# Two FFNs with seven block products for eight, one weight sum made by an accumulating transfer

## The chip, the cores and the metric

The kernel runs on one core of a Trainium2 chip. The metric is device time in microseconds of one execution, median of several. The core has five engines that each run their own instructions in order and wait for one another through semaphores: TensorE (PE, matmuls), VectorE (DVE), ScalarE (ACT), GpSimd (POOL) and SyncE (SP). Transfers are carried by 16 DMA engines; here SP issues the weight loads and GpSimd the small ones.

## The reference

One block of a streaming encoder: 256 frames of width 2048, all float32.

```python
x = x + 0.5 * swiglu_ffn(rmsnorm(x, norm_ffn1_g), ffn1_w_gate, ffn1_w_up, ffn1_w_down)   # 2048 -> 5632 -> 2048
proj = rmsnorm(x, norm_mix_g) @ w_in                                                     # 2048 -> 11264
...            # chunked band attention, chunkwise retention, gates, output projections
x = x + merged @ w_out
x = x + 0.5 * swiglu_ffn(rmsnorm(x, norm_ffn2_g), ffn2_w_gate, ffn2_w_up, ffn2_w_down)
return rmsnorm(x, norm_final_g)

def swiglu_ffn(x, w_gate, w_up, w_down):
    return (jax.nn.silu(x @ w_gate) * (x @ w_up)) @ w_down
```

Nearly all of the work is in the products of a 256-row activation with weight matrices that are each read once. The change touches the products with `w_gate` and `w_up` of the two FFNs.

## The kernel before

**Products.** A float32 product is made of three matmuls on a rounded type (fp32r): each operand is split into a high part (its rounding) and a low part (the rest), and high·high, high·low and low·high are summed in PSUM (L125 to L127). The weights are streamed in chunks of 2 x 128 rows by 512 columns, 512 KB each. For a chunk SP issues one load (`raw`, L94), ACT writes the high part (`hi`, L107), DVE subtracts to get the low part (`lo`, L108), and PE runs 12 matmuls of 512 columns: 2 row blocks by 2 frame halves by 3. A `Gemm` is a run of chunks that end in one 256x512 result in two PSUM banks.

**Order.** The order of each engine is that in which the program is written. `run` goes through the list of chunks; at each it first splits a few chunks ahead (`split_upto`), then runs what is due at this step (transposes, norms, attention pieces), then the chunk's matmuls, then what follows a finished `Gemm` (`done`). There are 4 buffers for `raw` and 5 each for `hi` and `lo`. An FFN makes 6 column blocks of 512 of the middle activation, each by a gate `Gemm` and an up `Gemm` of 8 chunks, then a part of the down product, then the other 5 blocks and the rest of the down product. There are 11 blocks in an FFN.

**Around it.** After a gate `Gemm` ACT takes SiLU out of PSUM (L374), after an up `Gemm` DVE multiplies (L379); the result is transposed on PE and split (L263, L264). After a down `Gemm` DVE adds to x (L357). The normed input is transposed and split by `Norm.put` (L322, L326, L330). x itself is loaded in quarters at the start, the last one at step 2 (L173).

## Time and profile before

| | us |
|---|---|
| median of 3 runs | 2179.64 (2179.56 to 2180.44) |
| the profiled execution, its own time | 2180.46 |
| its span, first to last instruction | 2178.4 |
| PE busy | 2167.7 |
| DVE busy | 1121.6 |
| ACT busy | 963.0 |
| GpSimd busy | 21.6 |

The granted TensorE clock of the profiled execution was 0.999 of full speed. Matmuls overlap in the records: one of 512 columns is shown with 0.39 us, while the next one starts 0.23 us later, so time is read from the starts. An instruction of DVE or ACT is likewise shown with its whole latency, and in a run of instructions the next starts a little before the end of the last.

### The profile page before, as it was taken

Reading aid. Unit: us, or ns where it says so; the run is one execution under the profiler, and the core shown is the slowest. Engines: PE = TensorE matmul, PEld = TensorE weight load, DVE = VectorE, ACT = ScalarE, POOL = GpSimd, SP = SyncE. Lnnn points to the kernel's source line nnn. Section 1 sums busy time; section 2 is a strip of 40 time slices with the busy share of each in tenths; the row PEclk is TensorE's granted clock in tenths of the full one; section 3 lists DMA queues with packets and bytes.
Section 4 is the critical chain, followed back from the end, with each engine's and each line's share of the span. In section 5 each row is a group of like instructions: output and inputs, shape, how many; then the busy total and the mean of one; then the engine's idle time right before and its main releaser. Section 6 shows DMA issues by size and latency. Waiting matters only on the chain.

```text
span 2178.4 us, 25308 instructions
## 1 busy us (share of the span) xinstructions
PE 2167.7 (100%) x9865; PEld 1802.5 (83%) x9865; DVE 1121.6 (51%) x1192; ACT 963.0 (44%) x1104; POOL 21.6 (1%) x36
## 2 busy tenths in 40 slices
PE   9999999999999999999999999999999999999998
PEld 7888888888888888888888888888888888888887
DVE  5544554445545544556655555554544544444554
ACT  6444433444444444454444444454444433444443
POOL 0000000000000000000000000000000000000000
PEclk9999999999999999999999999999999999999999
DMA  7655655666665555555555555556656556666554
GB/s 253 208 188 187 222 192 194 212 188 190 187 209 184 184 190 187 175 163 178 167 177 190 188 192 192 185 183 194 193 184 193 189 194 212 189 192 191 186 192 137
DMA packets 213512, 414.51 MB, mean 190 GB/s; under 512 B 12864, under 2 KB 13616, under 8 KB 213392
## 3 DMA queue, kind: packets, MB, share of 16 engines
q1 hardware_dynamic: 211424, 406.90, 57.9%
q0 software_dynamic: 1824, 5.93, 0.9%
q8 instruction: 77, 1.26, 0.2%
q14 instruction: 43, 0.35, 0.0%
q10 hardware_dynamic: 144, 0.07, 0.0%
HBM read 409.17 MB, written 3.67 MB: 190 GB/s over the span
## 4 chain that ended last, share of the span: by engine, by line
PE 99%; issue 0%; DMA 0%; ACT 0%; DVE 0%; POOL 0%; POOLq 0%; ACTq 0%
PE acc L125 32%; PE acc L126 32%; PE acc L127 32%; PE f2a0p L269 0%; PE f1a0p L269 0%; PE n1p L322 0%; DMA grows<-in_norm_ffn_g_dram 0%; PE f2a6p L269 0%; PE f1a6p L269 0%; PE mgp L269 0%; PE nmp L322 0%; PE n2p L322 0%; PE as L479 0%; PE rs L537 0%; PE av L514 0%
## 5 line engine op out<-in xcount | busy, mean ns | idle before, releaser
L108 DVE TENSOR_TENSOR lo<-raw,hi 128x1024 fp32r<-128x1024 f32 (+1 forms) x769 | 938.8, 1223 | 1014.0 <-ACT hi L107 1013.6
L107 ACT CAST hi<-raw 128x1024 fp32r<-128x1024 f32 (+1 forms) x769 | 808.2, 1052 | 1106.8 <-PE acc L127 1081.8
L125 PE MATMUL acc<-hi,nmh 128*128 128x512 f32 x704 | 277.8, 395 | 0.0
L125 PE MATMUL acc<-hi,n1h 128*128 128x512 f32 x704 | 276.2, 392 | 0.0
L125 PE MATMUL acc<-hi,n2h 128*128 128x512 f32 x704 | 274.8, 390 | 0.0
L126 PE MATMUL acc<-lo,n1h 128*128 128x512 f32 x704 | 274.7, 390 | 0.0
L127 PE MATMUL acc<-hi,n1l 128*128 128x512 f32 x704 | 274.6, 390 | 0.0
L127 PE MATMUL acc<-hi,nml 128*128 128x512 f32 x704 | 274.5, 390 | 0.0
L126 PE MATMUL acc<-lo,nmh 128*128 128x512 f32 x704 | 274.1, 389 | 0.0
L127 PE MATMUL acc<-hi,n2l 128*128 128x512 f32 x704 | 274.0, 389 | 0.0
L126 PE MATMUL acc<-lo,n2h 128*128 128x512 f32 x704 | 273.9, 389 | 0.0
L127 PEld LDWEIGHTS acc<-hi,n1l 128*128 128x128 f32 x704 | 132.4, 188 | 27.6
L127 PEld LDWEIGHTS acc<-hi,nml 128*128 128x128 f32 x704 | 132.2, 188 | 27.9
L125 PEld LDWEIGHTS acc<-hi,n1h 128*128 128x128 f32 x704 | 132.6, 188 | 27.3
L126 PEld LDWEIGHTS acc<-lo,n1h 128*128 128x128 f32 x704 | 132.4, 188 | 27.3 <-DVE lo L108 0.4
L127 PEld LDWEIGHTS acc<-hi,n2l 128*128 128x128 f32 x704 | 132.2, 188 | 27.5
L126 PEld LDWEIGHTS acc<-lo,n2h 128*128 128x128 f32 x704 | 132.2, 188 | 27.1
L125 PEld LDWEIGHTS acc<-hi,n2h 128*128 128x128 f32 x704 | 132.2, 188 | 27.0
L126 PEld LDWEIGHTS acc<-lo,nmh 128*128 128x128 f32 x704 | 132.3, 188 | 26.2
L125 PEld LDWEIGHTS acc<-hi,nmh 128*128 128x128 f32 x704 | 132.3, 188 | 26.2
L125 PE MATMUL acc<-hi,f2a0h 128*128 128x512 f32 x192 | 74.8, 390 | 0.0
L125 PE MATMUL acc<-hi,f1a0h 128*128 128x512 f32 x192 | 74.8, 389 | 0.0
(266 smaller groups left out, 2107.3 us busy)
## 6 DMA issues: line engine op xcount, KB each, us to landing
raw<-in_ffn_w_up_dram SPq DMA_DIRECT2D x176, 512.0 KB, 3.5
raw<-in_ffn_w_down_dram SPq DMA_DIRECT2D x176, 512.0 KB, 3.6
raw<-in_w_in_dram SPq DMA_DIRECT2D x176, 512.0 KB, 3.5
raw<-in_ffn_w_gate_dram SPq DMA_DIRECT2D x175, 512.0 KB, 3.5
raw<-in_w_out_dram SPq DMA_DIRECT2D x32, 512.0 KB, 3.7
raw<-in_w_out_att_dram SPq DMA_DIRECT2D x16, 512.0 KB, 4.3
raw<-in_w_out_ret_dram SPq DMA_DIRECT2D x16, 512.0 KB, 4.3
xall<-in_x_dram SPq DMA_DIRECT2D x3, 512.0 KB, 7.5
```

The costliest lines, as they stand in the source:

```text
L107: nc.scalar.copy(hi[:, p, :], raw[:, p, :])
L108: nc.vector.tensor_sub(lo[:, p, :], raw[:, p, :], hi[:, p, :].bitcast(F32))
L125: nc.tensor.matmul(acc, ahi[:, ts], whi[:, cs], start=first, stop=False)
L126: nc.tensor.matmul(acc, ahi[:, ts], wlo[:, cs], start=False, stop=False)
L127: nc.tensor.matmul(acc, alo[:, ts], whi[:, cs], start=False, stop=last)
```

## The change

In both FFNs the gate and up products of column blocks 1 to 10 are made together, as a 2 x 2 by 2 x 2 block product with seven products in place of eight. A is the normed activation: two frame halves of 128 rows, and the 2048 inner rows in two interleaved halves. B has gate and up as its two block columns, and the same inner halves: B11 and B21 are parts of gate, B12 and B22 of up. The sums are

- of A, made once per norm (`add_up`): s5, s7, s6, s3;
- of B, made for each block (`Strassen.step`): T1 = B11 + B12, T2 = T1 + B22, T2 - B11, T4 = T2 + B21.

A block is a group of 16 steps in four phases of four (`jc` 0 to 3), each step on a piece of 256 rows by 512 columns of each block: phase 0 multiplies a00·B11 and s5·T1, phase 1 s6·T2 and s3·B22, phase 2 s7·(T2 - B11) and a01·B21, phase 3 a11·T4. So a step of phases 0 to 2 has two weight operands, 12 matmuls, two `hi` and two `lo`; one of phase 3 has one operand and 6 matmuls. Standard chunks (up of block 0, then down) are woven in between, one at each D of `WOVEN`; a group with its D steps is `ppppD ppDppD pDpDpDpD ssssD`.

**T1** is made by a transfer: GpSimd issues a DMA from the tile with B11 (`k`) to the tile with B12 (`x`) that adds (L478). The other sums are DVE instructions: L513 (T2), L517 (T2 - B11), L521 (T4). B11 and B12 are kept in 8 tiles of the activation pool (`KEPT`), 4 `k` and 4 `x`; these are all that one group needs, and the next group's loads take the tiles as phases 2 and 3 free them.

Other edits: `hi` and `lo` have 4 buffers each, not 5, and a step's split waits until there is room for all its operands; PSUM has 4 banks for `acc`, 2 for `std`, 2 for `side`, where it had 4 and 4; some attention tiles move to the activation pool; the norms write a scaled copy first and split from that; the last `Gemm` keeps 2 steps (`TAIL`), not 4, for its three closing parts.

Three places of the order matter below. In names, `z104` is a group (that of block 5 of the first FFN), `z104k0` and `z104x0` are its tiles of `jc` 0, and `hiz104130` is the `hi` of group `z104`, phase 1, `jc` 3, operand 0.

ACT before, where one `Gemm` ends and chunks of later ones are split:

```order
L107 CAST hi58_1315<-raw58_1247 128x1024
L107 CAST hi59_1333<-raw59_1265 128x1024
L374 ACTIVATE f1g30_1351<-acc48_0_1195,n1rstd_88 128x512
L374 ACTIVATE f1g31_1353<-acc48_1_1196,n1rstd_88 128x512
L107 CAST hi60_1355<-raw60_1283 128x1024
L107 CAST hi61_1375<-raw61_1301 128x1024
```

ACT now, from the last step of phase 0 to the first two of phase 1:

```order
L498 CAST hiz104031_2604<-z104x3_2479 128x1024
L114 CAST hi108_2621<-raw108_2482 128x1024
L553 ACTIVATE z104s1_2639<-z104a_2567,n1rstd_88 128x512
L553 ACTIVATE z104s5_2641<-z104c_2574,n1minus_89 128x512
L498 CAST hiz104100_2644<-rawz10410_2484 128x1024
L498 CAST hiz104101_2647<-z104x0_2364 128x1024
L498 CAST hiz104110_2669<-rawz10411_2486 128x1024
```

Two copies out of PSUM stand ahead of the splits of phase 1, as two stood ahead of a later chunk's split before; what now follows them is only one D step ahead of PE.

DVE before, in a gate `Gemm`, one instruction to a chunk:

```order
L108 TENSOR_TENSOR lo38_925<-raw38_836,hi38_924 128x1024
L108 TENSOR_TENSOR lo39_943<-raw39_854,hi39_942 128x1024
L108 TENSOR_TENSOR lo40_961<-raw40_874,hi40_960 128x1024
L108 TENSOR_TENSOR lo41_979<-raw41_894,hi41_978 128x1024
L108 TENSOR_TENSOR lo42_997<-raw42_928,hi42_996 128x1024
```

DVE now, from the last step of phase 1 to the first of phase 2:

```order
L513 TENSOR_TENSOR z104x3_2479<-z104x3_2479,rawz10413_2652 128x1024
L501 TENSOR_TENSOR loz104130_2734<-rawz10413_2652,hiz104130_2733 128x1024
L501 TENSOR_TENSOR loz104131_2737<-z104x3_2479,hiz104131_2736 128x1024
L115 TENSOR_TENSOR lo114_2756<-raw114_2677,hi114_2755 128x1024
L561 SCALAR_TENSOR_TENSOR z104s2_2773<-z104c_2574,n1minus_89,z104s2_2773 128x512
L517 TENSOR_TENSOR z104k0_2362<-z104x0_2364,z104k0_2362 128x1024
L521 TENSOR_TENSOR z104x0_2364<-z104x0_2364,rawz10420_2695 128x1024
L501 TENSOR_TENSOR loz104200_2779<-rawz10420_2695,hiz104200_2778 128x1024
L501 TENSOR_TENSOR loz104201_2782<-z104k0_2362,hiz104201_2781 128x1024
L115 TENSOR_TENSOR lo116_2789<-raw116_2718,hi116_2788 128x1024
```

A D step has one of these instructions, a step of phase 1 three and one of phase 2 four, and the reading of a PSUM bank (L561) stands between the phases.

SP before, at the start:

```order
L94 DMA raw5_157<-in_ffn1_w_gate_dram 128x2x512
L94 DMA raw6_177<-in_ffn1_w_gate_dram 128x2x512
L94 DMA raw7_206<-in_ffn1_w_gate_dram 128x2x512
L173 DMA xall_77<-in_x_dram 128x2x512
L94 DMA raw8_234<-in_ffn1_w_up_dram 128x2x512
```

SP now:

```order
L108 DMA raw7_221<-in_ffn1_w_gate_dram 128x2x512
L108 DMA z8k0_223<-in_ffn1_w_gate_dram 128x2x512
L108 DMA z8x0_225<-in_ffn1_w_up_dram 128x2x512
L108 DMA z8k1_228<-in_ffn1_w_gate_dram 128x2x512
L108 DMA z8x1_230<-in_ffn1_w_up_dram 128x2x512
L108 DMA z8k2_233<-in_ffn1_w_gate_dram 128x2x512
L108 DMA z8x2_235<-in_ffn1_w_up_dram 128x2x512
L108 DMA z8k3_238<-in_ffn1_w_gate_dram 128x2x512
L108 DMA z8x3_240<-in_ffn1_w_up_dram 128x2x512
L219 DMA xall_77<-in_x_dram 128x2x512
```

The last quarter of x, which followed chunk 7, now follows the eight kept tiles of the first group.

The diff, cut to what these parts speak of:

```diff
 MASKED = -1e30
 
 RAW_BUFS = 4
-SPLIT_BUFS = 5
-ACT_TILES = 26
-TAIL = 4
+SPLIT_BUFS = 4
+KEPT = 8
+ACT_TILES = 30
+TAIL = 2
 AHEAD = (2, 3)
+BY_DMA = ("T1",)
+HALF_K = D // P // 2
+LEAD = 8
+EARLY = 3
+WOVEN = "ppppD" "ppDppD" "pDpDpDpD" "ssssD"
+WOVEN_LAST = "pDppDpD" "pDpDpDpD" "pDpDpDpD" "ssDssD"
 WARM = (6, 3)
 TAIL_PARTS = ((0, slice(0, NB)), (1, slice(0, NB // 2)), (1, slice(NB // 2, NB)))
...
+        def __call__(self, k, t):
+            ts = slice(t * P, (t + 1) * P)
+            return self.hi[k // 4][:, k % 4, ts], self.lo[k // 4][:, k % 4, ts]
...
+                if self.sums:
+                    nc.vector.tensor_scalar_mul(self.minus, self.rstd, -1.0)
+
+        def split_to(self, key, js, src):
+            if key not in self.part:
+                self.part[key] = [
+                    apool.tile([P, HALF_K, P], F32R, tag="act", name=f"{self.name}{key}{i}") for i in "hl"
+                ]
+            hi, lo = self.part[key]
+            nc.scalar.copy(hi[:, js, :], src)
+            nc.vector.tensor_sub(lo[:, js, :], src, hi[:, js, :].bitcast(F32))
...
+            j = 4 * (b // 2) + 2 * half
+            for t in range(NT):
+                src = raw[:, 2 * half : 2 * half + 2, t * P : (t + 1) * P]
+                self.split_to(f"a{t}{b % 2}", slice(j, j + 2), src)
+                    for n in range(2):
+                        later(1 + n, lambda n=n: self.add_up(b // 2, n))
...
+        def add_up(self, p, n):
...
+                s5, s7, s6, s3 = self.f
+                nc.vector.tensor_sub(s5, a22, a21)
+                nc.vector.tensor_sub(s7, a11, a21)
+                nc.vector.scalar_tensor_tensor(s6, s5, -1.0, a11, op0=ALU.mult, op1=ALU.subtract)
+                nc.vector.scalar_tensor_tensor(s3, s6, -1.0, a12, op0=ALU.mult, op1=ALU.subtract)
+            for i in (2 * n, 2 * n + 1):
+                self.split_to(self.SUMS[i], slice(4 * p, 4 * p + 4), self.f[i])
...
+    class Strassen:
...
+        def steps(self):
+            return [self.step(phase, jc) for phase in range(4) for jc in range(HALF_K // KC)]
...
+            def load_first():
+                self.kept[jc] = kept_tile("k")
+                fetch(self.kept[jc], self.w[0], self.rows(0, jc), self.col[0])
+
+            def load_second():
+                self.x[jc] = kept_tile("x")
+                fetch(self.x[jc], self.w[1], self.rows(0, jc), self.col[1])
+                if "T1" in BY_DMA:
+                    nc.gpsimd.dma_start(self.x[jc], self.kept[jc], accum_op=ALU.add)
+
+            def load_raw():
+                made["raw"] = weights_tile(f"raw{name}")
+                i = 2 - phase
+                fetch(made["raw"], self.w[i], self.rows(1, jc), self.col[i])
...
+            def two(first, second):
+
+                tiles = []
+                for i, raw in enumerate((first, second)):
+                    hi = wpool.tile([P, KC, NB], F32R, tag="hi", bufs=SPLIT_BUFS, name=f"hi{name}{i}")
+                    lo = wpool.tile([P, KC, NB], F32R, tag="lo", bufs=SPLIT_BUFS, name=f"lo{name}{i}")
+                    nc.scalar.copy(hi, raw)
+                    tiles.append((raw, hi, lo))
+                for raw, hi, lo in tiles:
+                    nc.vector.tensor_sub(lo, raw, hi.bitcast(F32))
+                return [(hi, lo) for _, hi, lo in tiles]
+
+            def prep():
+                x = self.x[jc]
+                if phase == 0:
+                    if "T1" not in BY_DMA:
+                        nc.vector.tensor_add(x, x, self.kept[jc])
+                    made["w"] = two(self.kept[jc], x)
+                elif phase == 1:
+                    raw = made["raw"]
+                    if "T2" not in BY_DMA:
+                        nc.vector.tensor_add(x, x, raw)
+                    made["w"] = two(raw, x)
+                elif phase == 2:
+                    raw, k = made.pop("raw"), self.kept.pop(jc)
+                    nc.vector.tensor_sub(k, x, k)
+                    if "T4" in BY_DMA:
+                        nc.gpsimd.dma_start(x, raw, accum_op=ALU.add)
+                    else:
+                        nc.vector.tensor_add(x, x, raw)
+                    made["w"] = two(raw, k)
+                else:
+                    made["w"] = [split(self.x.pop(jc), name)]
+
+            def products():
+                w = made["w"]
+                if phase == 0:
+                    self.product("a", "a00", jc, w[0], True, False)
+                    self.product("c", "s5", jc, w[1], True, False)
+                elif phase == 1:
+                    self.product("a", "s6", jc, w[1], False, False)
+                    self.product("c", "s3", jc, w[0], False, True)
+                elif phase == 2:
+                    self.product("a", "s7", jc, w[1], False, False)
+                    self.product("b", "a01", jc, w[0], True, True)
+                else:
+                    self.product("a", "a11", jc, w[0], False, True)
+                if jc == n - 1:
+                    self.end(phase)
+
+            loads = [("kept", load_first), ("kept", load_second)] if phase == 0 else [("raw", load_raw)]
+            frees = [[], ["raw"], ["raw", "kept"], ["kept"]][phase]
+            return Step(self, 0, loads if phase < 3 else [], prep, frees, 1 if phase == 3 else 2, products,
+                        early if phase == 1 and "T2" in BY_DMA else None)
+
+        def end(self, phase):
+
+            norm, acc, copy = self.norm, self.acc, self.copy
+
+            def copied(key, bank, scale):
+                copy[key] = tmp_tile(f"{self.name}{key}", "qk", 4)
+                nc.scalar.activation(copy[key], acc[bank], AF.Copy, scale=scale)
+
+            if phase == 0:
+                copied("s1", "a", norm.scale(0))
+                copied("s5", "c", norm.minus_scale(1))
+            elif phase == 1:
+                copied("s2", "a", norm.minus_scale(0))
+                r = copy["s2"]
+                nc.vector.scalar_tensor_tensor(r, acc["c"], norm.minus_scale(0), r, op0=ALU.mult, op1=ALU.add)
+                self.evict(0, 1, r)
+            elif phase == 2:
+                r = copy["s5"]
+                nc.vector.scalar_tensor_tensor(r, acc["a"], norm.minus_scale(1), r, op0=ALU.mult, op1=ALU.add)
+                self.evict(1, 1, r)
+                r = copy["s1"]
+                nc.vector.scalar_tensor_tensor(r, acc["b"], norm.scale(0), r, op0=ALU.mult, op1=ALU.add)
+                self.evict(0, 0, r)
+            else:
+                self.evict(1, 0, None, acc["a"])
...
+        queue = plain(0)
+        for pair in range((nblocks + 1) // 2):
+            queue += down(pair)
+        queue = [(job, k) for job in queue for k in range(0, job.nk, KC)]
+
+        def next_standard(n):
+            for job, k in queue[:n]:
+                steps.append(standard(job, k))
+            del queue[:n]
+
+        next_standard(LEAD)
+        for b in range(1, nblocks):
+            group = paired(b).steps()
+            for what in WOVEN if b < nblocks - 1 else WOVEN_LAST:
+                if what == "D":
+                    next_standard(1)
+                else:
+                    steps.append(group.pop(0))
+            assert not group
+        next_standard(len(queue))
+
+    n1 = Norm("n1", gains[:, 0, :], True)
+    nm = Norm("nm", gains[:, 1, :], False)
+    n2 = Norm("n2", gains[:, 2, :], True)
```

336 lines of the change are left out of this document (216 added, 120 removed).

## The prediction, as it was written before the changed kernel was run

> **What bounds the kernel now.** I read the page's busy times first, then the chain of waits that ended last.
>
> ```profile
> PE 2167.7 (100%) x9865; PEld 1802.5 (83%) x9865; DVE 1121.6 (51%) x1192; ACT 963.0 (44%) x1104; POOL 21.6 (1%) x36
> PE 99%; issue 0%; DMA 0%; ACT 0%; DVE 0%; POOL 0%; POOLq 0%; ACTq 0%
> ```
>
> PE sets the end; DVE and ACT work half the time. Third, the timeline of a stretch in the first FFN (start, duration, engine, line; idle before in brackets), which gives the rhythm and the hand-overs.
>
> ```profile
> 702.38 0.39 PE L125 MATMUL acc<-hi,f1a6h 128*128 128x512 f32 x1
> 702.58 1.05 ACT L107 CAST hi<-raw 128x1024 fp32r<-128x1024 f32 x1 [1.67 <-PE acc L127]
> 702.61 0.39 PE L126 MATMUL acc<-lo,f1a6h 128*128 128x512 f32 x1
> ...
> 703.67 1.23 DVE L108 TENSOR_TENSOR lo<-raw,hi 128x1024 fp32r<-128x1024 f32 x1 [1.50 <-ACT hi L107]
> ...
> 705.10 0.39 PE L125 MATMUL acc<-hi,f1a6h 128*128 128x512 f32 x1
> ```
>
> Twelve matmuls start between 702.38 and 705.10: 2.72 us a chunk, 0.227 us a matmul. ACT starts 0.20 us after PE has gone on from the chunk that held its buffer; DVE starts 0.04 us after ACT's end (702.58 + 1.05 = 703.63). Each chunk needs 1.23 us of DVE in 2.72. How dense DVE and ACT can go is seen where several follow one another (x is their count, the duration is of all):
>
> ```profile
> 36.53 1.26 ACT L374 ACTIVATE f1g<-acc,n1rstd 128x512 f32<-128x512 f32 x2
> 37.69 2.95 ACT L107 CAST hi<-raw 128x1024 fp32r<-128x1024 f32 x3
> 38.77 4.63 DVE L108 TENSOR_TENSOR lo<-raw,hi 128x1024 fp32r<-128x1024 f32 x4 [3.15 <-ACT hi L107]
> 56.66 1.40 DVE L379 SCALAR_TENSOR_TENSOR f1g<-acc,n1rstd,f1g 128x512 f32<-128x512 f32 x2
> ```
>
> In a row a DVE instruction of 1024 takes (4.63 - 1.23)/3 = 1.14 us. The groups by line and shape give the rest (busy, mean ns of one):
>
> ```profile
> L379 DVE SCALAR_TENSOR_TENSOR f1g<-acc,n1rstd,f1g 128x512 f32<-128x512 f32 x22 | 15.4, 743 | 0.0
> L357 DVE SCALAR_TENSOR_TENSOR xall<-acc,xall 128x512 f32<-128x512 f32 x38 | 24.4, 682 | 0.0
> L374 ACT ACTIVATE f1g<-acc,n1rstd 128x512 f32<-128x512 f32 x22 | 15.0, 689 | 9.9 <-PE acc L127 9.9
> ```
>
> So in a row 0.66 us (1.40 - 0.74) for a scaled eviction on DVE, 0.60 for the other ones of 512 (0.68 less the same 0.08), and 0.57 for one on ACT (1.26 - 0.69).
>
> **What PE loses.** Twenty groups (ten a FFN) have 168 matmuls each where two Gemms had 192: 480 x 0.227 = 108.8 us off the chain that sets the end. With nothing else this gives 2180.5 - 108.8 = 2071.7 on the profiled execution's own time.
>
> **What DVE gains.** A group has 28 splits for 16, and 12 sums (T2, T2 - B11, T4; four of each): 24 more instructions of 1024, 480 in all, 547 us at 1.14. That fits into the whole span, but it falls into the groups. A group with its 8 D steps, put-in-middle included, phase by phase:
>
> - phase 0 (`ppppD`): PE 5 x 2.72 + 8 transposes (0.87, row below) = 14.5. DVE 9 x 1.14 + 3 x 0.60 + 2 x 0.60 = 13.3.
> - phase 1 (`ppDppD`): PE 16.3. DVE 14 x 1.14 + 0.66 = 16.6.
> - phase 2 (`pDpDpDpD`): PE 21.8. DVE 20 x 1.14 + 2 x 0.60 = 24.0.
> - phase 3 (`ssssD`): PE 8.2. DVE 5 x 1.14 + 2 x 0.66 + 0.60 = 7.6.
>
> ```profile
> 104.69 0.87 PE f1a0p L269 x8
> ```
>
> PE 60.8 us, DVE 61.5: DVE goes from half busy to as busy as PE. Nor can it save up time: `hi` and `lo` have four buffers and a step takes two, so it is at most two steps (5.4 us) ahead, less where a buffer comes free late. Three waits are then PE's.
>
> 1. Phase 0 to 1. ACT reads both banks before it splits for phase 1, and the second closes with PE's last product of phase 0. From there 0.20 + 0.57 (second eviction) + 1.05 (`hi`) + 0.04 + 1.14 (first `lo`) + 1.23 (second, which the product takes first) + 0.04 = 4.27 us; PE has a D step and one matmul, 2.72 + 0.23 = 2.95, so it waits 1.3. In the next step DVE's sum and two `lo` take 1.14 + 1.14 + 1.23 = 3.5 against 2.72: 0.8 more. Together 2.1.
> 2. Phase 1 to 2. L561 stands ahead of phase 2's instructions on DVE and waits for the end of phase 1; behind it are T2 - B11, T4 and both `lo`, and for these PE: 0.20 + 0.66 + 3 x 1.14 + 1.23 + 0.04 = 5.55, less 2.95, 2.6.
> 3. Phase 2 itself: 24.0 - 21.8 = 2.2.
>
> Phase 3 costs nothing extra, since its evictions stand behind the first `lo` of the phase and PE has a D step and that step's 1.36 us meanwhile. A group thus takes 60.8 + 6.9 = 67.7 us, and 20 groups add 138. A bound from below is each phase at its longer engine, 14.5 + 16.6 + 24.0 + 8.2 = 63.3, 2.5 a group. From above, every extra semaphore that stands on DVE's way could cost its 0.04 on some 40 instructions, 1.6 us a group, 32 in all. I take 138, because the waits follow from the order of single engines.
>
> **T1 by transfer.** It takes four DVE instructions, 4.6 us, out of each group, else DVE would be at 66. GpSimd is free for it. Its price is not in the trace; the nearest rows are GpSimd's transfers of the same 512 KB, beside the weights' queue (median us to landing):
>
> ```profile
> q1 hardware_dynamic: 211424, 406.90, 57.9%
> raw<-in_ffn_w_up_dram SPq DMA_DIRECT2D x176, 512.0 KB, 3.5
> biasT<-rel_ext POOLq DMA_DIRECT2D x2, 512.0 KB, 6.1
> decay<-in_decay_dram POOLq DMA_DIRECT2D x2, 512.0 KB, 7.1
> ```
>
> The queue moves 406.9 MB in 57.9% of 2178 us, 323 GB/s, so reading the target as well adds 1.6 us: 7.7 to 8.7. Below it is 6.1, a plain one; above 14.2, both ends done in turn. The cover: the group's last kept tile is free when phase 3's last `lo` ends; up to the fourth x of the next phase 0 DVE has eight more instructions of 1024 and five of 512, 12.1 us, less ACT's 1.1; 3.5 go to the load, 7.5 are left. At 8.7 it is 1.2 late, which phase 0's surplus (14.5 - 13.3) takes in. So I cost it at nothing, but without that cover each us is 20.
>
> [...]
>
> **Start, end, the rest.** x's last quarter is now behind eight kept tiles on SP.
>
> ```profile
> 17.40 0.46 SPq L173 DMA_DIRECT2D xall<-in_x_dram  x1
> L322 PE MATMUL n1p<-id_sb,xall x32: 270/272/476, 6.0 to 29.6; 128*128 128x128 f32 x32
> DMA to landing us min/median/max: 4.1/5.5/9.4
> ```
>
> Eight tiles are 4.2 MB, 13 us at 323 GB/s. Before, it was issued at 17.4 and landed 4 to 9 us later; its transposes stand shortly before 29.6, so 4 us or so are spare and PE waits about 9 (0 if the loads go faster, 13 without any slack). The first groups also have the sums of A on DVE, about 16 instructions of 512 (10 us) a norm, under the first eight chunks in which DVE has 12 us free: I take 4 for both norms (0 to 20). At the end two steps in place of four halve the cover of the closing work, parts of 2.7 us become 1.36: 2 us (0 to 3). The mixer's moved tiles and PSUM banks lie under PE at DVE 50% busy: nothing, at most a copy of 0.6 us at each of a few transposes.
>
> Sum: 2180.5 - 108.8 + 138 + 9 + 4 + 2 = 2224.7. The median of the runs is 0.8 below the profiled execution, so **2224 us**, 2.0% slower.
>
> **The rivals.**
>
> A. The waits don't come, and a group ends at its longer engine phase by phase: 2071.7 + 50 + 15 = 2137, faster. For it: ACT has 40% of a group to spare (36 casts of 0.95 and some 6 us of evictions in 67), and DVE's sums are ready early. Against: L561 and the evictions stand in order ahead of what PE needs next. At 2 us of wait a group in place of 6.9 it is still faster; the sides change at 4.7 (108.8 - 15 over 20).
>
> B. T1 lands late. At 14.2 us it is 6.7 late, 5.5 after the slack, and all of it is PE's: 2224 + 110 = 2334; at 11 us, half way, 2270. For it: no row shows the price, and the next group's tiles are loaded only when this one frees them. Against: 6.1 and 7.1 for a like transfer.
>
> C. The waits shrink by a third, as PE's and DVE's delays overlap: 20 x 4.7 + 15 - 108.8 = 0, about 2180, no change.
>
> D. The clock. PE now stands still for up to 2.6 us at a time, and after an idle start it runs at half speed:
>
> ```profile
> 10.20 0.63 PE L127 MATMUL acc<-hi,n1l 128*128 128x512 f32 x1
> 10.62 0.63 PE L125 MATMUL acc<-hi,n1h 128*128 128x512 f32 x1
> core 0: 2178.4 us, clock 0.999
> ```
>
> 0.42 us from start to start, against 0.23. If one such wait a group brought 3 us at half speed, as the start has, that is 1.5 x 20 = 30: 2254. [...]
>
> **How the numbers follow.** The forecast's mechanism 0.61, with its own range 2205 to 2250; B 0.17; A 0.10; C 0.07; D 0.05. Eight in ten reach from 2190 (the forecast with 5.2 us of waits a group) to 2290 (T1 at 12 us). Repeated runs here differ by 0.04%, and I call a change told from none at 0.2%, 4.4 us. Faster: A and a third of C, 0.12; same: a third of C and a little of the edges, 0.04; slower: the rest, 0.84.
>
> **What would show it.** In the groups' stretches DVE at 90% or more busy, PE's matmul starts with gaps; by the waits PE's matmuls released by DVE `lo` of L501, most time at the first step of phase 2 (2.6 us each), then phase 1 (1.3 and 0.8); a period of 67 to 68 us from one group's first product to the next one's. ACT's `hi` of x waiting for GpSimd's DMA would show B; a granted clock under 0.98 D; a period under 65 A. A gap of some 9 us near 26 us would bear out the start. The forecast is wrong if DVE has idle time between the phases that PE does not share.

## The result, and the profile after

The changed kernel takes **2314.6 us** (2309.4 to 2315.4) against 2179.6: 1.0614 times as long, 95% interval 1.0595 to 1.0632. The direction was forecast, the size was not: 2224 was the number and 2290 the upper end. Executions of one kernel agree within 0.5%, except one of experiment 2 at 7446 us, which its ratio leaves out. The profiled execution has a span of 2313.6 us; its page gives busy times and the chain of waits that ended last:

```profile
PE 2156.8 (93%) x9337; PEld 1732.8 (75%) x9337; DVE 1742.8 (75%) x1830; ACT 1243.1 (54%) x1468; POOL 90.5 (4%) x116
PE 57%; DVE 19%; DMA 11%; issue 6%; ACT 4%; SPq 0%; POOL 0%; ACTq 0%; DVEq 0%; POOLq 0%
```

PE went from 100% of the span to 93% and from 99% of the chain to 57%. That DVE would stand in the chain was forecast; the **11% of DMA** was not. In one group, from its first product at 564.8 us to the next one's at 636.8 (72.0 us, forecast 67.7), the view of waits (who waited for what: us in all, times, longest) says for PE:

```profile
PE z176a L123 <- DVE loz L501: 3.7, 3, 1.9
PE z176c L122 <- ACT hiz L498: 1.8, 1, 1.8
PE z176c L123 <- DVE loz L501: 0.8, 1, 0.8
PE z176a L122 <- ACT hiz L498: 0.5, 1, 0.5
```

the same view for DVE:

```profile
DVE loz L501 <- ACT hiz L498: 6.8, 3, 4.6
DVE z176s L561 <- PE z176c L124: 1.8, 1, 1.8
...
```

and for ACT, among others:

```profile
...
ACT hiz L498 <- DMA z176x<-z176k: 5.0, 1, 5.0
...
```

This row is the sign named for rival B: ACT stands 5.0 us for an adding transfer, DVE 4.6 us behind ACT, and PE pays 1.8 + 0.8 at the fourth product of s5 (gaps of 1.9 and 1.03 us between matmul starts, 9.4 us into the group). DVE stands 2 us longer there than PE; idle time of DVE that PE doesn't share was the forecast's own sign of being wrong. The first and fourth rows of PE are the forecast waits. By matmul starts these are, in a group without late T1 (of experiment 2 below), 1.22 + 0.70 (forecast 1.3 + 0.8), 0.63 + 2.17 (2.6) and 1.42 (2.2): 6.1 us for 6.9.

Why T1 is late shows in the group at 493.6 us. The transfers of its kept tiles (KB each, median us to landing):

```profile
z152k<-in_ffn_w_gate_dram SPq DMA_DIRECT2D x4, 512.0 KB, 8.1
z152x<-in_ffn_w_up_dram SPq DMA_DIRECT2D x4, 512.0 KB, 8.8
z152x<-z152k POOLq DMA_DIRECT2D x4, 512.0 KB, 9.4
```

The medians hide the last load. Of the loads of x and the additions into them the view of their tile says, from issue to landing:

```profile
DMA to landing us min/median/max: 6.5/9.3/16.0
```

The queues between 470 and 505 us (packets, MB, share of the 16 engines):

```profile
q1 hardware_dynamic: 3657, 7.03, 56.1%
q0 software_dynamic: 576, 2.10, 30.1%
```

GpSimd's timeline there:

```profile
480.33 0.86 POOL L478 DMA_DIRECT2D z152x<-z152k  x1 [54.99 <-DMA z152x<-in_ffn_w_up_dram]
482.94 0.86 POOL L478 DMA_DIRECT2D z152x<-z152k  x1 [1.76 <-DMA z152x<-in_ffn_w_up_dram]
485.64 0.86 POOL L478 DMA_DIRECT2D z152x<-z152k  x1 [1.84 <-DMA z152x<-in_ffn_w_up_dram]
495.81 0.86 POOL L478 DMA_DIRECT2D z152x<-z152k  x1 [9.31 <-DMA z152x<-in_ffn_w_up_dram]
```

The transfer itself takes about what was estimated (9.4 for 7.7 to 8.7; the medians of the twenty groups are 8.5 to 10.0). What is late is what it adds to: SP issues the eight kept loads in a row between 472.7 and 479.2, and the last x, issued at 479.2, lands at 495.3, 16 us later, where 3.5 were assumed. In these 35 us a load takes 0.561 x 35 / 13.4 = 1.5 us of all 16 engines (7.03 MB are 13.4 loads) and an adding transfer 0.301 x 35 / 4 = 2.6. The first three additions run while the last loads wait, and between them they hold up the fourth's operand: GpSimd stands 9.3 us for it. The fourth T1 lands at 503.3, 24.0 us after the load was issued.

The cover, the time from that load's issue to the use of the tile, is not as it was forecast either. The last load is issued when the last `lo` of phase 2 has ended (478.00 + 1.22), not the last of phase 3, which ends 8.8 us later (484.49 + 3.50):

```profile
478.00 1.22 DVE L501 TENSOR_TENSOR loz<-z128k,hiz 128x1024 fp32r<-128x1024 f32 x1
479.24 0.37 SPq L108 DMA_DIRECT2D z152x<-in_ffn_w_up_dram  x1
484.49 3.50 DVE L115 TENSOR_TENSOR loz<-z128x,hiz 128x1024 fp32r<-128x1024 f32 x3 [0.25 <-ACT hiz L114]
```

At the start the wait for x's last quarter is 16.2 us where 9 were forecast (view of one tile: who waited for x, us, times):

```profile
  DMA xall<-in_x_dram: 16.2, 1
```

The granted clock is 0.972 in place of 0.999. DVE is busy 87% of two groups (125.4 of 144.1 us, row in experiment 4), under the 90% that the forecast named.

### The profile page after: what moved, and what is told of

It reads as the page before. It is cut to its first block, busy times and chain, and to the rows that moved or that the text cites. A ratio compares the mean times of both kernels' runs of the same rounds, so it can differ in the third digit from the quotient of the medians.

```text
span 2313.6 us, 25633 instructions
## 1 busy us (share of the span) xinstructions
PE 2156.8 (93%) x9337; PEld 1732.8 (75%) x9337; DVE 1742.8 (75%) x1830; ACT 1243.1 (54%) x1468; POOL 90.5 (4%) x116
## 3 DMA queue, kind: packets, MB, share of 16 engines
q1 hardware_dynamic: 211424, 406.90, 55.1%
## 4 chain that ended last, share of the span: by engine, by line
PE 57%; DVE 19%; DMA 11%; issue 6%; ACT 4%; SPq 0%; POOL 0%; ACTq 0%; DVEq 0%; POOLq 0%
PE acc L122 13%; PE acc L124 13%; PE acc L123 13%; DVE loz L501 7%; ACT hiz L498 3%; DVE lo L115 3%; DVE xall L587 1%; DMA z128x<-z128k 1%; DMA z632x<-z632k 1%; DMA z512x<-in_ffn_w_up_dram 1%; DMA z56x<-in_ffn_w_up_dram 1%; DMA z104x<-in_ffn_w_up_dram 1%; DMA z704x<-in_ffn_w_up_dram 1%; DMA z680x<-z680k 1%; DMA z584x<-in_ffn_w_up_dram 1%
## 5 line engine op out<-in xcount | busy, mean ns | idle before, releaser
L115 DVE TENSOR_TENSOR lo<-raw,hi 128x1024 fp32r<-128x1024 f32 (+1 forms) x449 | 545.7, 1220 | 311.5 <-ACT hi L114 310.7
L114 ACT CAST hi<-raw 128x1024 fp32r<-128x1024 f32 (+1 forms) x449 | 469.6, 1047 | 346.6 <-PE acc L124 312.5
L501 DVE TENSOR_TENSOR loz<-rawz,hiz 128x1024 fp32r<-128x1024 f32 x160 | 195.1, 1219 | 33.2 <-ACT hiz L498 33.2
L498 ACT CAST hiz<-rawz 128x1024 fp32r<-128x1024 f32 x160 | 167.1, 1045 | 57.5 <-PE acc L124 29.8
L122 PE MATMUL acc<-hi,nma00h 128*128 128x512 f32 x176 | 70.6, 401 | 0.0
L122 PE MATMUL acc<-hi,nma01h 128*128 128x512 f32 x176 | 70.1, 398 | 0.0
L124 PE MATMUL acc<-hi,nma00l 128*128 128x512 f32 x176 | 68.7, 390 | 0.0
L124 PE MATMUL acc<-hi,nma01l 128*128 128x512 f32 x176 | 68.6, 390 | 0.0
L122 PE MATMUL acc<-hi,nma10h 128*128 128x512 f32 x176 | 68.6, 390 | 0.0
L123 PE MATMUL acc<-lo,nma00h 128*128 128x512 f32 x176 | 68.6, 390 | 0.0
```

Source lines behind the costliest of these rows:

```text
L114: nc.scalar.copy(hi[:, p, :], raw[:, p, :])
L115: nc.vector.tensor_sub(lo[:, p, :], raw[:, p, :], hi[:, p, :].bitcast(F32))
L122: nc.tensor.matmul(acc, ahi, whi, start=first, stop=False, **more)
L123: nc.tensor.matmul(acc, ahi, wlo, start=False, stop=False, **more)
L124: nc.tensor.matmul(acc, alo, whi, start=False, stop=last, **more)
L498: nc.scalar.copy(hi, raw)
```

## The experiments

Each is an edit of the changed kernel; before takes 2178.6 to 2179.4 us beside them.

**1. T1 on DVE.**

```diff
-BY_DMA = ("T1",)
+BY_DMA = ()
```

> B11+B12 is made by DVE in place of the adding transfer; nothing is left out. Theory 1 (the fourth T1 of a group lands 2 to 3 us late, and that is what the transfer costs): the PE wait of 1.2 to 2.2 us + 1.03 at 9.4 us into a group goes (-3.0 x 20 = -60 us), but DVE has 4 x 1.14 = 4.6 us more in phase 0, 17.9 against PE's 14.5, so +3.4 x 20 = +68: 2300 to 2330 us, no verdict on the transfer as a whole, but the waits of ACT hiz on z..x go. Theory 2 (the loads and the weights' queue are what is slow, and T1 is only the place where it shows): the gap at 9.4 us stays and DVE's load comes on top: 2380 us. Theory 3 (DVE has slack in phase 0, the forecast's DVE count is too high): 2250 us.

Measured: 2303.1 us, 1.0566 (1.0550 to 1.0582), 0.5% **faster** than with the transfer. ACT waits for no adding transfer any more; a group takes 71.55 us. The row of the stretch 554.5 to 626.1 (length; busy us and instructions of PE, its weight loads, DVE, ACT, GpSimd; clock; DMA share; GB/s):

```profile
554.50:626.10 71.60, 64.08 (x275) 49.62 (x274) 67.27 (x64) 40.00 (x43) 0.00 (x0) 1.00 0.51 176
```

DVE is busy 94% of it. Theory 1 holds: two prices of the same size.

The loads are issued here as in the changed kernel, eight in a row, with no addition beside them. From issue to landing the four of `z152x` take:

```profile
DMA to landing us min/median/max: 6.4/8.8/9.9
```

The last takes 9.9 us in place of 16.0. So of the 12.5 us over the assumed 3.5 the loads among themselves make 6.4, and the group's first three additions 6.1.

**2. No T1.** The sum is left out, so the s5 product takes B12 alone.

```diff
-                if "T1" in BY_DMA:
-                    nc.gpsimd.dma_start(self.x[jc], self.kept[jc], accum_op=ALU.add)
```

> T1 is left out: neither transfer nor DVE makes B11+B12, so the product that should take the sum takes B12 alone. Theory 1 (late T1 costs 3 us a group, and the clock falls after it): the gap at 9.4 us goes, -60 us, and with it the half-clock windows that follow it, 12 or so of the 25 at some 1.7 us each, -20: 2235 us, a group at 68 to 69. Theory 2 (the fourth x is late because eight loads of 512 KB stand in a row, transfer or not): the gap shrinks by less than half, 2285 us or more. Theory 3 (the clock falls for the waits at phase 2 alone): the gap goes, the number of half-clock windows stays, 2255 us.

> The kernel without T1 once more (neither transfer nor DVE makes B11+B12; the product that should take the sum takes B12 alone), for its trace: it took 2250 us. Theory 1: the gap at 9.4 us of a group is gone, the waits at 0 to 1 (1.2 + 0.7), 1 to 2 (0.6 + 2.2) and in phase 2 (1.4) stay, a group takes 68.5 us, and the half-clock windows that are left follow the wait at phase 2. Theory 2: the gap is there, smaller, and ACT's hiz waits for the load.

Measured: 2250.3 us, 1.0322 (1.0305 to 1.0340), and 2249.0 in a single further execution, whose trace is read here. PE's waits in a group and its stretch:

```profile
PE z176a L123 <- DVE loz L499: 4.6, 4, 1.9
PE z176a L122 <- ACT hiz L496: 0.5, 1, 0.5
...
537.70:606.00 68.30, 63.06 (x274) 49.81 (x272) 62.53 (x60) 40.42 (x44) 0.00 (x0) 1.00 0.54 185
```

The gap at 9.4 us is gone and the forecast's waits are left, with a group at 68.35 us; DVE is busy 92% of it. **All that the transfer of T1 costs is 2314.6 - 2249.0 = 65.6 us.** Nothing waits for T1 here, so the trace shows the cover, from the issue of the group's last load to the `hi` of its fourth x:

```profile
454.67 0.37 SPq L108 DMA_DIRECT2D z152x<-in_ffn_w_up_dram  x1
474.77 1.06 ACT L496 CAST hiz<-z152x 128x1024 fp32r<-128x1024 f32 x1 [0.30 <-PE z152c L124]
```

These are 20.1 us, where the forecast had 12.1 - 1.1 = 11.0; from the last `lo` of phase 3, where it began to count, they are 11.3. In the changed kernel load and addition take 24.0, 4 us more than the cover. Part of the 65.6 is at the start: x's last quarter is waited for 8.8 us here (and in experiment 1), not 16.2, so 7.4 come from the first group's adding transfers, which are in flight beside it (x's quarter is issued at 23.4 us, they from 25.3 on).

**3. x's last quarter first.**

```diff
     load_x(2 * NB, 3 * NB)
+    load_x(3 * NB, 4 * NB)
 ...
-    at(2, lambda: load_x(3 * NB, 4 * NB))
```

> x's last quarter is loaded right behind its third, ahead of the eight kept tiles. Theory 1 (the quarter behind the kept tiles costs the 16.2 us that PE waits for it): -16 us, less up to 1.6 us by which the kept tiles come later: 2297 us. Theory 2 (the start's loads are bound by bandwidth, the wait only moves to the chunks or the first T1): within 4 us of 2314.

Measured: 2301.3 us, 1.0558 (1.0543 to 1.0574): 13.3 of the 16.2 us. PE has no wait for x, and the first group starts at 41.4 us in place of 53.4.

**4. Matmuls in the waits.**

```diff
+FILL = (4, 7)
 ...
+                    if jc == n - 1:
+                        self.fill(FILL[0])
                     self.product("c", "s5", jc, w[1], True, False)
 ...
-                    self.product("a", "s7", jc, w[1], False, False)
+                    self.product("a", "s7", jc, w[1], False, False, FILL[1] if jc == 0 else 0)
```

`fill(n)` issues n matmuls of 512 columns into a bank that is not yet in use; in the call of `product` they stand behind its first matmul.

> Matmuls that need no new data go into two of the waits of a group and write a bank that is not yet in use: 4 (0.9 us) ahead of the fourth x's product of phase 0, 7 (1.6 us) between the first product's hi and lo at phase 2. 220 matmuls more, 50 us of PE's work. Theory 1 (the granted clock falls to a half for 3.41 us after a stretch of 3.41 us in which PE stood still for 2.0 us or more; the fillers lie in waits and cost nothing): almost no half-clock windows between 70 and 2300 us, which have cost some 45 us; DVE has used some of it to catch up, so -25 to -45: 2270 to 2290 us. Theory 2 (the clock falls for another reason, such as power, with the load): it falls as often or more, 2314 us or more. Theory 3 (the waits are not waits for data, fillers come on top): +50, 2365 us.

What it tests is seen in the changed kernel in three stretches of 3.41 us, behind late T1 of the group above:

```profile
574.83:578.24 3.41, 1.16 (x4) 0.77 (x5) 1.94 (x2) 2.58 (x3) 0.00 (x0) 1.00 0.00 0
578.24:581.65 3.41, 3.41 (x10) 2.63 (x9) 1.99 (x3) 2.09 (x3) 0.00 (x0) 0.50 0.49 145
581.65:585.07 3.42, 3.35 (x15) 2.42 (x14) 3.42 (x4) 1.69 (x3) 0.00 (x0) 1.00 0.39 114
```

PE stands for most of the first, runs at half clock in the second, at full in the third. Laid out from the trace's clock changes and matmul starts, 632 such stretches at full clock lie between 30 us and the end: in the 28 that are followed by half clock PE stood 1.99 us or more, in the 604 others at most 2.09.

Measured: 2312.6 us, 1.0613 (1.0597 to 1.0628): no difference from the change. The two groups from 564.8 to 708.9 in the changed kernel:

```profile
564.80:708.90 144.10, 131.54 (x547) 103.03 (x545) 125.40 (x119) 80.02 (x87) 6.85 (x8) 0.96 0.68 207
```

and the same stretch with the fillers (its two groups lie from 566.0 to 708.7):

```profile
564.80:708.90 144.10, 133.87 (x578) 104.85 (x577) 126.25 (x120) 80.65 (x87) 6.85 (x8) 1.00 0.67 210
```

The clock is 1.00 here in place of 0.96, and 0.988 over the span in place of 0.972: it goes with PE's standing still, as theory 1 has it, and the fillers cost nothing (2312.6 us against 2314.6); but the 25 to 45 us that I expected of it don't come. The half-clock stretches stand in a group whose end DVE sets: while PE is slow, DVE gets ahead, and a later wait shrinks (by matmul starts the 1.22 us wait of phase 1 is 0.24 behind the half-clock stretch above, and the 1.42 us wait in phase 2 is missing where such a stretch stands ahead of it). Experiment 6 shows this more closely.

**5. The eviction at phase 1's end a step later.**

```diff
-                nc.vector.scalar_tensor_tensor(r, acc["c"], norm.minus_scale(0), r, op0=ALU.mult, op1=ALU.add)
-                self.evict(0, 1, r)
+                def close():
+                    nc.vector.scalar_tensor_tensor(r, acc["c"], norm.minus_scale(0), r, op0=ALU.mult, op1=ALU.add)
+                    self.evict(0, 1, r)
+
+                later(1, close)
```

> The eviction of c at the end of phase 1 (L561 on DVE) is issued a step later, so that T2-B11, T4 and the two lo of phase 2's first step and the lo of the D step stand ahead of it. Theory 1 (the wait at phase 1 to 2 comes from that order): DVE no longer idles 1.85 us there, and the PE waits of 0.6 + 2.2 us go, of which DVE's 0.66 for the eviction comes back in phase 2: between -1.85 x 20 = -37 and -2.8 x 20 = -56, 2258 to 2277 us. Theory 2 (DVE's amount of work sets the group, and the wait only moves on to the next steps of phase 2): 2300 us or more.

Measured: 2273.0 us, 1.0431 (1.0416 to 1.0447), -41.6. DVE's wait at L561 is gone; PE's waits in a group:

```profile
PE z176a L123 <- DVE loz L501: 2.3, 3, 1.3
PE z176c L122 <- ACT hiz L498: 1.4, 1, 1.4
PE z176c L123 <- DVE loz L501: 0.8, 1, 0.8
```

The 0.63 + 2.17 at phase 2's first step become 0.88 at a later one: 1.9 us less a group, of the 2.1 (41.6 / 20) that were gained, as theory 1 has it (DVE's 0.66 comes back). The wait that the forecast priced highest is a matter of order on one queue.

**6. k0, x0, k1, x1 loaded earlier.**

```diff
+    for i in range(LEAD, len(transfers) - 7):
+        rings = "".join(r[0] for r, _ in transfers[i : i + 10])
+        if rings == "rrkkkkkkkk":
+            d3, d4, *kept = transfers[i : i + 10]
+            transfers[i : i + 10] = kept[:2] + [d3] + kept[2:4] + [d4] + kept[4:]
```

> The loads of a group's first two pairs of kept tiles are issued two and one places earlier on SP: k0, x0 ahead of the last two standard tiles of the group before, k1, x1 between them. Same bytes, same transfers. Theory 1 (T1 is late because eight loads and four adding transfers share 16 engines within 25 us; the adding transfer takes 2.7 to 2.9 us of all of them, a load 1.35): about 5 us of it are done before the bunch, the fourth T1 lands 4 us earlier and the gap of 1.2 to 2.2 + 1.03 us goes: 2255 to 2275 us. Theory 2 (the adding transfer's own 7.5 to 10 us is what is late): the last load is as late as before, 2300 us or more.

Measured: 2267.1 us, 1.0400 (1.0382 to 1.0417), -47.5. PE's waits in a group, and two groups' stretches, each from its first product to the next one's:

```profile
PE z176a L123 <- DVE loz L501: 3.4, 3, 1.9
PE z176a L122 <- ACT hiz L498: 0.5, 1, 0.5
...
549.30:617.70 68.40, 64.52 (x276) 51.10 (x273) 62.64 (x61) 40.58 (x44) 3.43 (x4) 0.98 0.69 216
1800.90:1869.30 68.40, 63.18 (x276) 49.91 (x274) 62.63 (x61) 40.52 (x44) 3.44 (x4) 1.00 0.68 215
```

The same bytes and the same 80 additions, and late T1 is gone: 68.35 us, what a group takes without T1. An addition takes here about what it took before (group medians of 7.4 to 9.1 us); the last load of `z152x` lands after 9.7 us in place of 16.0, and load and addition together take 18.6, inside the cover of 20.1. So the lateness was the **bunch**, loads and additions on the same engines at once, not the transfer's own time: in experiment 1 the same loads, alone, land early enough to leave an addition its time, and here the same additions come in time with the loads spread. And the group with a half-clock stretch (0.98) takes as long as that without (1.00), 68.4 us each: the clock costs nothing here.

**7. T4 on GpSimd.**

```diff
-                        nc.vector.tensor_add(x, x, raw)
+                        nc.gpsimd.tensor_add(x, x, raw)
```

> The sum T4 of phase 2 (four of 128x1024 a group) is made by GpSimd in place of DVE. Theory 1 (DVE's work sets phase 2): 4 x 1.14 = 4.6 us less for DVE, the wait in phase 2 (1.4) goes and that at phase 1 to 2 falls by 1.1: -2.5 x 20 = -50, 2265 us. Theory 2 (only the order at the hand-overs costs): -1.1 x 20 = -22, 2293 us. Theory 3 (DVE runs slower while GpSimd works on the same memory, or GpSimd's sum comes too late for phase 3): 2315 us or more.

Measured: 2369.3 us, 1.0872 (1.0855 to 1.0888), 55 us slower. The groups by line (busy, mean ns of one | idle before): GpSimd's sum, and the `lo` that DVE makes beside it:

```profile
L521 POOL TENSOR_TENSOR z176x<-z176x,rawz 128x1024 f32<-128x1024 f32 x4 | 12.4, 3098 | 40.2 <-DVE z176k L517 32.1 <-ACT hiz L498 4.7 <-DMA rawz<-in_ffn_w_gate_dram 3.5
...
L501 DVE TENSOR_TENSOR loz<-z176k,hiz 128x1024 fp32r<-128x1024 f32 x8 | 15.7, 1956 | 0.5 <-ACT hiz L498 0.3
```

The same `lo` in the changed kernel:

```profile
L501 DVE TENSOR_TENSOR loz<-z176k,hiz 128x1024 fp32r<-128x1024 f32 x8 | 9.7, 1218 | 0.0
```

The mean of 1956 mixes two kinds. Five of the eight take 1.22 us, three take 3.0 to 3.3, each beside a sum on GpSimd; the first pair in the timeline:

```profile
617.13 3.20 POOL L521 TENSOR_TENSOR z176x<-z176x,rawz 128x1024 f32<-128x1024 f32 x1 [32.05 <-DVE z176k L517]
...
618.16 3.26 DVE L501 TENSOR_TENSOR loz<-z176k,hiz 128x1024 fp32r<-128x1024 f32 x1
```

Theory 3. In these three the subtraction ends 1.09 us behind the sum, near the 1.14 of one in a row, as if it had waited the sum out. In the whole kernel 62 subtractions of L501 are that long, 2.0 us over their 1.22 each, 124 us; what DVE saves is 80 x 1.14 = 91. T1 is no later with this edit: ACT waits 90 us in all for adding transfers, 96 in the changed kernel. How the 55 us come out of these 33 more of DVE's time isn't taken apart.

**8. The three edits 3, 5 and 6 together.**

> The three edits that each made it faster, together: k0, x0, k1, x1 loaded earlier (alone -47.5 us), the eviction of c a step later (-41.6), x's last quarter ahead of the kept tiles (-13.3). Theory 1 (they take away different waits): the gains add up, 2314.6 - 102.4 = 2212 us, a group at 66.3. Theory 2 (behind them stands DVE's amount of work in phase 2, which takes part of it back): 2225 to 2240 us.

Measured: 2212.9 us, 1.0152 (1.0136 to 1.0167); the sum of the single gains gave 2212. A group:

```profile
521.60:588.00 66.40, 62.87 (x274) 49.81 (x273) 62.45 (x60) 40.44 (x44) 3.42 (x4) 1.00 0.71 222
```

The three gains add up, so the three edits take away different waits. DVE is busy 94%.

**9 and 10. T4 by transfer too, and T4 alone by transfer**, both on top of 8.

```diff
-BY_DMA = ("T1",)
+BY_DMA = ("T1", "T4")        # 9
+BY_DMA = ("T4",)             # 10
```

> As the kernel with the three edits, and the sum T4 of phase 2 is made by an adding transfer too. Theory 1 (DVE's work in phase 2 is what is left: it falls by 4.6 us a group, and the waits of 1.4 and 0.9 us there go): -2.3 x 20 = -46 against the three, 2166 us, and faster than the kernel before. Theory 2 (80 more transfers that take 2.8 us of all 16 engines each collide with the kept tiles' loads and with T1, which comes late again): no gain, 2212 us or more. Theory 3 (the transfer holds the raw buffer longer than DVE did, and the four raw buffers run out): PE waits for raw loads in phase 2, 2230 us or more.

> As the kernel with the three edits, but DVE makes T1 and an adding transfer makes T4. Theory 1 (each sum costs what DVE's queue has room for at its place): T1 on DVE brings the waits of 1.9 + 0.7 in phase 0, +51, T4's transfer takes away 2.3 a group, -46: 2217 us. Theory 2 (as T4 has more time before it is needed than T1, the transfer is hidden, and DVE, freed in phase 2, comes into phase 0 earlier): 2180 to 2200 us.

Measured: 2313.5 us, 1.0617 (1.0598 to 1.0636), and 2296.9, 1.0549 (1.0530 to 1.0567): both far above 8. What ACT waits for in a group of 9:

```profile
ACT hiz L114 <- DMA z176x<-rawz: 6.2, 2, 3.9
```

and of 10:

```profile
ACT hi L114 <- DMA raw<-in_ffn_w_down_dram: 5.7, 1, 5.7
```

In 9 T4's transfers fall into the bunch of the next group's loads and are late for phase 3; in 10 a standard tile's load is. For the transfer's price: of the two T4 of the group at 487.5 us in 9 that are issued at 517.3 and 523.5, the shorter lands after 4.8 us; the group medians of T4's transfers are 5.9 and 6.1 us in the last group of each FFN, behind which no kept tiles are loaded, and 6.6 to 10.0 in the others. My expectation of -46 us for 9 costed the transfer at nothing, the mistake of the prediction once more, and both theories of 10 (2217, and 2180 to 2200) miss.

**11. Five pairs of hi and lo**, on top of 8, with 28 act tiles for 30.

```diff
-SPLIT_BUFS = 4
+SPLIT_BUFS = 5
-ACT_TILES = 30
+ACT_TILES = 28
```

> As the kernel with the three edits (2212.9 us), with five pairs of hi and lo in place of four, and 28 act tiles in place of 30 to make room. A step of a group takes two pairs and a standard step one, so with five the splits of the next phase's first step can stand ahead of the evictions at a phase's end. Theory 1 (what is left of the hand-overs comes from there being no free pair before the evictions): the waits at phase 0 to 1 (1.22 + 0.71) and 1 to 2 (0.87) go, at most 2.8 x 20 = -56, and at least half of it as DVE's 62.7 us of work a group is near: 2157 to 2185 us. Theory 2 (with 28 act tiles the kept tiles' loads wait for a free one and T1 comes late again): 2212 us or more.

Measured: 2198.4 us, 1.0088 (1.0071 to 1.0105). Between the theories: the waits at phase 0 to 1 go, and groups of 63.5 us appear, but every second one takes 66 to 68, four of these six with T1 late (ACT waits 2.8 to 5.5 us for it), and one has a gap of 12.4 us.

**12. The relative bias's loads behind the last group's additions** (changed kernel otherwise).

```diff
+REL_AHEAD = 34
 ...
-    at(70, load_rel)
 ...
+    at(mix - REL_AHEAD, load_rel)
```

> The changed kernel with the four loads of the relative bias on GpSimd's queue moved behind the last group of the first FFN. Theory 1 (they stand between two adding transfers of the group at 273 us, wait for an act tile and hold up T1): that group comes down from 76.0 to 72, the one before loses its gap of 3.8 us at the end, -6 to -8 us in all: 2307 us. Theory 2 (the 16 engines alone set T1, the queue does not matter): 2313 to 2316 us.

In the changed kernel GpSimd's timeline has these loads between two additions:

```profile
256.17 0.92 POOL L478 DMA_DIRECT2D z80x<-z80k  x1 [52.81 <-DMA z80x<-in_ffn_w_up_dram]
256.76 3.19 POOL L263 DMA_DIRECT2D rel<-in_rel_bias_dram  x4
259.62 1.28 POOL L478 DMA_DIRECT2D z80x<-z80k  x1
273.78 0.87 POOL L478 DMA_DIRECT2D z80x<-z80k  x1 [12.88 <-DVE xall L587]
```

Measured: 2305.2 us, 1.0579 (1.0561 to 1.0597), -9.4: the two groups there go from 74.6 and 76.0 us to 71.3 and 71.7. Which of queue, engines and act tiles it is, this run doesn't separate. Experiment 2 does for a part: with no addition on the queue at all, the group at 260 us still takes 71.9 us, 3.6 more than the others, and ACT stands there as follows.

```profile
266.23 1.07 ACT L309 CAST f1a1h<-f1a1p 128x512 fp32r<-128x512 f32 x2 [5.39 <-PE z80c L124]
```

The transposes that it reads ended at 260.6; the semaphore on which it stands until 266.1 is that of the first transfer `rel_ext<-rel`, which lands at 266.08. So `f1a1h` waits for the act tile that the bias holds until it is written out.

**13, 14 and 15.** 13 is 11 with edit 12, and with edit 6 kept off the second FFN's first group. 14 has 29 act tiles (the squares' scratch shares a tag, and a pool of small tiles has 4 buffers for 8). 15 has DVE's negated 1/rms four steps later:

```diff
-                    nc.vector.tensor_scalar_mul(self.minus, self.rstd, -1.0)
+                    later(4, lambda: nc.vector.tensor_scalar_mul(self.minus, self.rstd, -1.0))
```

> The kernel with the three edits and five split pairs (2198.4 us), with the loads of the relative bias behind the last group, and without the earlier loads at the first group of the second FFN, where a gap of 9.4 us stood ahead of it. Theory 1 (these two places, and nothing else, cost 12.4 - 2 and 9.4 us, 3 to 4 more at the end of the group before): 2198.4 - 22 = 2176 us, level with the kernel before. Theory 2 (the bias's loads only collide with something else later, and the gap ahead of the second FFN is the norm's): 2190 us or more.

> As e13_five_rel, with 29 act tiles in place of 28 (the scratch of the squares shares a tag, which makes the room). Theory 1 (every second group takes 66.6 us in place of 63.5 because its kept tiles wait for a free act tile and T1 comes late): most of these groups come down, six by 3 us: -18, 2158 us, under the kernel before. Theory 2 (the act tiles do not set it): as e13_five_rel.

> As e14_five_29, but DVE's negated 1/rms (n1minus, n2minus), which waits for GpSimd's n2rstd, is issued four steps later, so that the splits do not stand behind it. Theory 1 (PE's 12.2 us at 1460 us come from GpSimd's queue by way of that instruction): -12 us, 2161 us. Theory 2 (the loads themselves are late there, and the splits wait for them anyway): 2170 us or more.

Measured: 13: 2187.0 us, 1.0038 (1.0023 to 1.0053). 14: 2173.0, 0.9976 (0.9966 to 0.9986). 15: **2162.8, 0.9927 (0.9913 to 0.9940), under the kernel before.** 13 misses its 2176: the groups came down by 18.7 us in sum, but the gap ahead of the second FFN grew from 9.4 to 14.9, so the earlier loads were not its cause. 14 lies between its theories (2158, and as 13): three groups come down by 2.5 to 3.1 us, the others by 1.3 or less. The gap is 12.3 us there, and the rows around 1460 us name its cause. PE's waits:

```profile
PE acc L124 <- DVE lo L116: 12.2, 1, 12.2
```

DVE's:

```profile
DVE n2minus L368 <- POOL n2rstd L307: 20.8, 1, 20.8
```

and GpSimd's timeline:

```profile
1457.18 0.85 POOL L479 DMA_DIRECT2D z512x<-z512k  x1 [4.14 <-DMA z512x<-in_ffn_w_up_dram]
1457.74 1.02 POOL L307 TENSOR_TENSOR n2rstd<-v,mhalf 128x2 f32<-128x2 f32 x1
```

GpSimd computes 1/rms right behind its fourth addition, which had waited for its load; DVE waits for 1/rms, and PE for the splits behind it on DVE. Taken out of the way (15), PE has one wait there, half as long:

```profile
PE z512a L124 <- DVE loz L502: 6.0, 1, 6.0
```

## Why the prediction was right or wrong

**Right:** the 480 matmuls are gone, and at full clock they still start every 0.227 us, so nothing speaks against PE's gain of 108.8 us. The three waits at the hand-overs were found at their places with nearly their sizes: experiment 2, which has nothing late from T1, shows groups of 68.35 us for 67.7. DVE's work of 61.5 us a group is 62.5 in its rows. The start's 9 us are 8.8 there.

**Wrong, the step that failed:** "3.5 go to the load, 7.5 are left. At 8.7 it is 1.2 late, which phase 0's surplus (14.5 - 13.3) takes in. So I cost it at nothing". The term that was mis-sized is the load: it takes 16.0 us, not 3.5. 3.5 us is the landing time of a load that is issued every 2.7 us, while here twelve loads are issued within 9 us, and the group's first three additions come on the same 16 engines behind them; 6.4 of the 12.5 us more are the loads' own, 6.1 the additions'. The cover was mis-sized too, but the other way: the last kept tile is free with phase 2's last `lo`, not phase 3's, and the cover is 20.1 us, not 11.0. So with a load of 3.5 us the answer "nothing" would have been right with some 7 us to spare; with 16.0 + 0.6 + 7.5 = 24 (load, issue, addition) T1 is 4 us late. That costs PE 3 us a group, and the start's quarter comes 7.4 late: 65.6 of the 90 us that the forecast lacks.

The transfer's own price came out near the estimate (group medians of 8.5 to 10.0 us for 7.7 to 8.7), but this is in part luck: the estimate was built on rows of 6.1 and 7.1 with no bunch beside them, and where no bunch follows, T4's additions land after 5.9 and 6.1 at the median (experiment 9). The 1.6 us in it for reading the target were an estimate that no run takes apart; what the queues show is 2.6 us of all 16 engines for an addition against 1.5 for a load. It is rival B in its place and sign (ACT's `hi` of x waits for GpSimd's DMA), at a price between its points of 2270 and 2334, but not by its reason, a slow transfer. A share of the whole span doesn't show the crowding: the additions' queue has 9.9% of the engines there, 0.9% of it from before, and the loads' queue 55.1%, but from 472.3 to 495.3 us they have 34.3% and 63.0%.

**The other 25 us:** 18 of the groups take 1245.0 us in experiment 2 where 67.7 each makes 1218.6, 26.4 more; 4 of it were in the forecast as the sums of A. 18 x 0.65 = 11.7 is the usual group at 68.35: its three waits are 0.8 under the forecast, and small waits of 0.1 to 0.2 come to some 1.4 (68.35 - 60.8 - 6.1), near the 1.6 that the forecast named as the bound from above and didn't take. The first group takes 75.6 and the second 70.1, 9.0 over 68.35, and the same two of the second FFN 1.7 over it: 10.7 us where the sums of A and their splits stand, for which I had 4. The group at 260 us takes 71.9, 3.6 more, for the act tile that the bias holds (experiment 12). The 2 or 3 us that are left aren't taken apart. "GpSimd is free for it" was wrong as well: its queue also carries the bias's loads and 1/rms, in the order of the program (experiments 12 to 15; in 14 1/rms starts at 1457.7 us, behind an addition that had stood 4.1 us for its load).

**Rival D** came true in its sign (the clock at 0.972, half-clock stretches in nearly every group) and not in its price: 30 us were named, experiments 4 and 6 show none that can be measured. In the changed kernel PE stood 1.99 us or more, in pieces, in each of the 28 stretches of 3.41 us that half clock follows, and at most 2.09 in the 604 others (experiment 4). **Rival A** said that the waits don't come, and they did; edits 5 and 11 make most of them go, and with T1 in time the change then is faster, as its turning point of 4.7 us of waits a group said: in 14 and 15 all but the first group of each FFN have 2.3 to 4.7 (gaps over 0.14 us between matmul starts, in sum).

## What to carry to other kernels

A transfer that replaces an engine's instruction is not priced by its own time but by its queue: add up what is in flight on the same DMA engines in the stretch before it is needed, its operand's load first and what earlier transfers of the same kind do to that load (here 9.9 us became 16.0), and take landing times from a stretch with that crowding; a median of four hides the last one (8.8 for 16.0 here). Check from a trace, too, when the buffer really comes free. Where two engines are level, look for the reads of a finished bank that stand in order ahead of the next phase's inputs, and for buffers that force them there: moving one such instruction by a step was worth 42 us, a fifth buffer some 14. Before an "idle" queue is given work that waits, list what else it issues and who waits for that.

## What was not expected of the hardware

- Of 632 stretches of 3.41 us at full clock, the 28 that were followed by one at half clock had PE standing 1.99 us or more in pieces, the other 604 at most 2.09. In a group whose end DVE sets, the half clock cost nothing (68.4 us with and without it in experiment 6).
- An adding transfer of 512 KB within SBUF took 4.8 us to land in one place of experiment 9, 6.4 to 13.4 in the changed kernel, and there 2.6 us of all 16 engines, against 1.5 for a load (470 to 505 us). Three of them behind a bunch of loads brought the landing of the last load from 9.9 to 16.0 us.
- A sum of two tiles of 128x1024 on GpSimd took 3.1 us, and a DVE subtraction that started beside it 3.0 to 3.3 in place of 1.22 (experiment 7).
